# Mixed small edits in a two-branch streaming encoder step: first tiles, weight copies in DRAM, closing norm

## The chip, the cores and the metric

The kernel runs on one core of a Trainium2 chip. The metric is the time of one execution on the device in microseconds (us), lower being better. Engine names are those of the profile: PE is TensorE, DVE is VectorE, ACT is ScalarE, POOL is GpSimd, SP is SyncE, which here only issues transfers. A line such as L1037 is a line of the kernel before.

## The reference

One layer is applied to two independent groups of frames: 512 frames of a new stream (the prompt) and 32 frames of a running one (the sample). Both go through the same weights, so the kernel joins them into 544 columns. Cut to what matters:

```
xn   = rmsnorm(x, norm_g)
proj = xn @ w_in            # u, v, z, gates, q, f, i, g, ga, gb
c    = silu(causal_conv(u));  q, k = c @ w_qm, c @ w_km   (4 heads of 512)
hm   = mLSTM(q, k, v, gates; C, n, m)  -> new C, n, m
oh   = HGRN2(q_h, f_h, i_h; S)         -> new S
y    = sigmoid(ga) * (hm' @ w_brm) + sigmoid(gb) * (oh' @ w_brh)
h    = x + y @ w_out
h    = h + sigmoid(h @ w_pg) * (p @ w_ple)
out  = rmsnorm(h, final_g)
```

All of it is float32. Outputs are out and the new states of both groups.

## The kernel before, in words

Activations lie with features on the 128 partitions and the 544 frames along the free axis, so x is eight tiles of 128 x 544 (KD = 8). To keep float32 precision in matmuls on rounded operands, every operand is split into a high part (a cast) and a low part (a subtraction), and three products are summed: high x high, high x low, low x high. ACT makes most of the high parts, DVE the low parts (split_piece, L127 to L135). Large weight matrices are paired and multiplied with seven in place of eight products (class Two).

The order of the work is set in two ways. In the first stage (L1397 to L1609) the orders of ACT, DVE and PE are those of the code. Behind it only PE's order is that of the code; the builder orders ACT, DVE, POOL and SP itself by its own estimate, within the data dependences. `tc.issue_after(x)` adds one rule: what is issued inside, on x's engine, comes behind x in its queue.

The first stage loops over the eight x tiles (L1413 to L1436). Each tile is scaled by norm_g and split (L1417, L1418), the first three columns of weights are split (wf), the tile is squared into sq for the sum of squares (L1426 or L1428), and products() issues PE's matmuls for the tile two before. ACT squares all tiles but 0 and 2, which POOL squares; POOL also adds the squares of tiles 0 and 1 and of 2 and 3 (L1431), and DVE adds the rest. `summed` is POOL's last of these adds. Behind it in POOL's queue stand the eight scalings of the sample's columns, xg (L1441), and further small copies that name `summed`: the edges of the convolution tiles (conv_edges, L257) and the ones behind the values (L1499, L1608).

The matrices w_out and w_pg are needed late, in sums and differences of their blocks. late_steps() makes these in DRAM: sixteen groups of four transfers of 256 KB each, all issued from POOL's queue, as plain copies or as accumulating ones. make_late(n, after) issues the next n groups, behind an instruction on POOL. Its places are stage_k (L985, behind the ksm copies of the sample's keys), stage_scores (L1024, for heads 0 and 1, behind the scaled queries qw) and the value part of heads 1 to 3. For head 0 that is one group in stage_k and one in stage_scores.

stage_decay reads a tile bc, a row of DRAM broadcast to 128 partitions by SP (decay_rows, L929 to L933). DVE adds the mask to it (dm, L943), POOL copies a piece of it to wi (L953), and qw is the queries times wi. The first score product, sc (L1037), takes a PSUM buffer that vq, the sample's values, had before; DVE's three vsum sums (L1616) read it out.

The last stage runs the w_pg product, adds the gated embeddings to h and squares it into total, in two halves of 272 columns. Then rms_cols takes the sum of squares of a half by six small matmuls (r10 for the first half, r11 for the second) and computes 1/sqrt by a short chain on DVE; norm_bcast spreads the result over the partitions with six matmuls (r1pb); norm_out scales the eight h tiles of that half, five on DVE (L2166) and three, the tiles 4, 5 and 6 called `aside`, on POOL (L2164), and sends each as one y transfer (L2167). Between these, PE makes the last head's new memory C (memories()): three blocks of four steps of six matmuls, then one block in two halves. C leaves through ACT's queue. TAIL says how many steps stand where:

```
next(rest)                        # one step
r = rms_cols(... one ...)         # r10
for _ in range(TAIL[0]): next(rest)
r1 = rms_cols(... other ...)      # r11
norm_out(0, norm_bcast(0, r))
for _ in range(TAIL[1]): next(rest)
norm_out(1, norm_bcast(1, r1))
```

Of the kernel before, what the change touches and what calls it, by code (L numbers as in the profile page):

```python
# [14 lines left out]
ALU = mybir.AluOpType  # L15
# [41 lines left out]
LASTBR = 2  # L57
WSPLIT = 256
U5, U7, U4, U6 = range(4)
TAIL = (4, 4)  # L60
FIRST = 1 << 24

V_FG, V_CW, V_CB, V_MG, V_SK, V_LB, V_HG, V_CS, V_GV = 0, 8, 72, 88, 104, 120, 136, 144, 192
# [4 lines left out]
def hybrid_step(ctx: ExitStack, tc: tile.TileContext, a, o):  # L68
# [29 lines left out]
    def half(b):  # L98
        return slice(b * TH, (b + 1) * TH)
# [126 lines left out]
    def rms_cols(acc, blocks, name, pc=None):  # L226

        pc = pc or paux(name + "pc")
        n = len(blocks)
        st = small("rms_s", [P, 8])  # L230
        V.memset(st[:, :n], 1.0)
        for i, (t0, m) in enumerate(blocks):
            PE.matmul(pc[:m, 0, 2 * i : 2 * i + 2], acc[:, t0 : t0 + m], ones, start=True, stop=True)
        i = 0
        while i < n:
            j = i
            while j < n and blocks[j][1] == blocks[i][1]:
                j += 1
            m = blocks[i][1]
            V.tensor_scalar(st[:m, i:j], pc[:m, 0, 2 * i : 2 * j : 2], 1.0 / D, EPS, ALU.mult, ALU.add)  # L240
            i = j
        r = small("rms_r", [P, 8])
        rsqrt(r[:, :n], st[:, :n], P, n)
        return r
# [169 lines left out]
    def make_late(n, after):  # L414

        with tc.issue_after(after.ins):
            for _ in range(n):
                next(late_sums)
# [545 lines left out]
    def stage_k(h):  # L964

        cs = st8[h]["cs"]
        kf, ks = [], []
        for u in range(2):
            w = st8[h].pop(f"wk{u}", None) or weight(a["w_km"][h, u], f"wk{h}{u}", eng=V if h else G)
            for f in range(2):  # L970
                acc = dense(w, f * P, 256, P, cs, f"k{h}{u}{f}")
                t = eslot(f"kf{h}{u}{f}")
                for b in range(2):
                    with tc.high_priority() if h else nullcontext():
                        read = S.mul(t[:, half(b)], acc[b], HD**-0.5)  # L975
                if u == 0:
                    first = read
                kf.append(t)
                kh, kl = slot(f"kh{h}{u}{f}", F32R), slot(f"kl{h}{u}{f}", F32R)
                n = NP - P if h else NP  # L980
                S.copy(kh[:, :n], t[:, NS : NS + n])
                V.tensor_tensor(kl[:, :n], t[:, NS : NS + n], kh[:, :n].bitcast(F32), ALU.subtract)
                ks.append((kh, kl))
        ksm, copied = triple(kf, "ksm")
        make_late(2 if h > 1 else 1, copied)  # L985
        st8[h].update(kf=kf, ks=ks, ksm=ksm, copied=copied)
        return first

# [28 lines left out]
    def stage_scores(h):  # L1017

        dj, ds, wi, ks, ksm, qs, qf, qw = (st8[h][k] for k in ("dj", "ds", "wi", "ks", "ksm", "qs", "qf", "qw"))
        kf, qx = st8[h]["kf"], st8[h].get("qx")  # L1020
        for i in range(KH):
            scaled = G.tensor_tensor(qw[:, i], qf[:, i * NS : (i + 1) * NS], wi, ALU.mult)
        if h < 2:
            make_late(1, scaled)  # L1024
        sh2, sl2 = slot(f"sh2{h}", F32R), slot(f"sl2{h}", F32R)
        st = []
        for j in range(NB):
            pn = paux(f"sc{h}{j}")
            n = NP - j * P
            for f in range(KH):  # L1030
                if h and j == NB - 1:
                    PE.matmul(
                        pn[:, 0, :n], kf[f][:, T - P : T], qx[:, f], start=(f == 0), stop=(f == KH - 1)
                    )
                    continue
                for i, (x, y) in enumerate(((0, 0), (0, 1), (1, 0))):
                    PE.matmul(  # L1037
                        pn[:, 0, :n],
                        ks[f][x][:, j * P : (j + 1) * P],
                        qs[f][y][:, NS + j * P : T],  # L1040
                        start=(f == 0 and i == 0),
                        stop=(f == KH - 1 and i == 2),
                    )
            with tc.high_priority():
                V.tensor_tensor(dj[j], pn[:, 0, :n], dj[j], ALU.mult)
            if j < 2:
                sh, sl = slot(f"sh{h}{j}", F32R)[:, :n], slot(f"sl{h}{j}", F32R)[:, :n]
            else:
                sh, sl = (x[:, (j - 2) * 256 : (j - 2) * 256 + n] for x in (sh2, sl2))
            with tc.high_priority():  # L1050
                S.copy(sh, dj[j])
                low = V.tensor_tensor(sl, dj[j], sh.bitcast(F32), ALU.subtract)
            st.append((sh, sl))
        pn = paux(f"scs{h}")
        for f in range(KH):
            PE.matmul(
                pn[: 3 * NS, 0, :NS],
                ksm[:, f],
                qf[:, f * NS : (f + 1) * NS],
                start=(f == 0),  # L1060
                stop=(f == KH - 1),
            )
        dss = small("dss", [3 * NS, NS], F32R)
        V.tensor_tensor(ds, pn[: 3 * NS, 0, :NS], ds, ALU.mult)
        V.tensor_copy(dss, ds)
        V.tensor_tensor(dss[2 * NS :], ds[2 * NS :], dss[2 * NS :].bitcast(F32), ALU.subtract)
        st8[h].update(st=st, dss=dss)
        return low
# [328 lines left out]
    with tc.manual_schedule(engines={mybir.EngineType.Activation, mybir.EngineType.DVE, mybir.EngineType.PE}):  # L1397
# [15 lines left out]
        for k in range(KD):  # L1413
            t = xt[k]
            hi, lo = pair_tile(f"x0{k}", k // (KD // 2))
            g = t[:, T : T + 1]
            S.mul(hi, t[:, :T], g)  # L1417
            V.scalar_tensor_tensor(lo, t[:, :T], g, hi.bitcast(F32), ALU.mult, ALU.subtract)  # L1418
            x0.append((hi, lo))
            wf[k].append(split_piece(wf[k][0], f"wf{k}", NF * P))  # L1420
            if k == 1:
                load(KD - 2)
                load(KD - 1)
            sqk = slot(f"r0q{k}")[:, :T]
            if k not in (0, 2):
                S.activation(sqk, t[:, :T], AF.Square)  # L1426
            else:
                G.tensor_tensor(sqk, t[:, :T], t[:, :T], ALU.mult)  # L1428
            sq.append(sqk)
            if k in (1, 3):  # L1430
                summed = G.tensor_tensor(sq[k - 1], sq[k - 1], sqk, ALU.add)  # L1431
            if k in (5, 6):
                i, j = ((0, 2), (4, 5))[k - 5]
                V.tensor_tensor(sq[i], sq[i], sq[j], ALU.add)
            if k > 1:
                products(k - 2)  # L1436
        for i, j in ((0, 4), (6, 7), (0, 6)):
            V.tensor_tensor(sq[i], sq[i], sq[j], ALU.add)
        with tc.issue_after(summed.ins):
            for k in range(KD):  # L1440
                G.tensor_scalar(xg[:, k], xt[k][:, :NS], xt[k][:, T : T + 1], None, ALU.mult)  # L1441
        raws = [raw_piece(a["w_in"][3][:, c : c + WP], f"wu3r{c}") for c in (0, WP)]
        w3 = [split_piece(raws[0], "wu30", WP, WSPLIT)]
        products(KD - 2)
# [701 lines left out]
    def norm_bcast(b, r):  # L2146
        pb = paux(f"r1pb{b}")
        for i, (t0, m) in enumerate(blocks):
            bcast(pb[:, 0, t0 : t0 + m], r, i, m)
        return pb  # L2150
# [7 lines left out]
    def norm_out(b, pb):  # L2158
        rows = slot(f"rows{b}")
        S.copy(rows[:, :TH], pb[:, 0, :TH])  # L2160
        for f in (0, 4, 1, 2, 5, 3, 7, 6):
            t = h1[f][:, half(b)]
            if f in aside:
                G.tensor_tensor(t, t, rows[:, :TH], ALU.mult)  # L2164
            else:
                V.scalar_tensor_tensor(t, t, vcol(V_FG + f), pb[:, 0, :TH], ALU.mult, ALU.mult)  # L2166
            nc.sync.dma_start(o["y"][f, :, half(b)], t)  # L2167

    def memories():
        for f in range(KH - 1):  # L2170
# [4 lines left out]
    with tc.manual_schedule(engines={mybir.EngineType.PE}):  # L2175
        pump = Pump(gates_)
        pump.prepare(2)
        h_sums(HK - 1)
        pump.to(2)
        for f in range(NB):  # L2180
            for i in range(2):
                nc.sync.dma_start(kw[f][i][:, :HD].bitcast(F32), kv_d[f, i, :, :HD])
                nc.sync.dma_start(vv[f][i][:, :VW].bitcast(F32), kv_d[NB + f, i, :, :VW])
        pump.end()
        rest = memories()
        next(rest)
        r = rms_cols(total[0][:, one], blocks, "r10")
        norm_scale()
        for _ in range(TAIL[0]):
            next(rest)  # L2190
        r1 = rms_cols(total[0][:, other], blocks, "r11")
        norm_out(0, norm_bcast(0, r))
        for _ in range(TAIL[1]):
            next(rest)
        norm_out(1, norm_bcast(1, r1))
        for _ in rest:
            pass
# [98 lines left out]
```

## Time and profile before

| | us |
|---|---|
| timed runs | 1104.68, 1108.60, 1108.76 |
| their median | 1108.6 |
| the profiled execution | 1106.54 |
| its span, first to last instruction | 1104.8 |
| PE busy in it | 1093.3 |
| DVE busy | 925.5 |
| ACT busy | 692.7 |
| POOL busy | 210.6 |

The profile is of one execution, whose own time stands in the table beside its span; durations and starts below are from it, counted from the span's start. The granted PE clock is 0.999 of full speed over the span. Rows of the timeline give start, duration, engine, line, operation, output and inputs, shapes and a count; idle time before a row stands in brackets, with what ended it by the profile's guess. Matmuls overlap each other, so a row of one can be longer than the distance to the next.

### The profile page before, as it was taken

The numbers are of one execution on the slowest core, as the hardware profiler recorded it, in microseconds if no ns is written. First come the engines' busy times: TensorE is split into PE (matmuls) and PEld (weight loads), VectorE is DVE, ScalarE is ACT, GpSimd is POOL, SyncE is SP. The second block draws the span as 40 slices with busy tenths as digits, with TensorE's granted clock in tenths as the row PEclk, the third lists the DMA queues.
The fourth block names the chain that finished last, engine by engine and source line by source line (L and its number), as shares of the span: only waits on it lengthen the run. The fifth ranks groups of instructions, "written<-read, shape, count | busy, mean of one in ns | idle before, by whom it ended". The sixth has DMA issues, their size and how long they took to land.

```text
span 1104.8 us, 23775 instructions
## 1 busy us (share of the span) xinstructions
PE 1093.3 (99%) x8625; PEld 1070.3 (97%) x8625; DVE 925.5 (84%) x2101; ACT 692.7 (63%) x1577; POOL 210.6 (19%) x376
## 2 busy tenths in 40 slices
PE   9999999999999999999999999999999999999997
PEld 8899999999999999999999999999999999999997
DVE  7889988676896795986888799999999977778885
ACT  6767557754666554765656477776776666446683
POOL 7204010303021031202220122322232210000001
PEclk9999999999999999999999999999999999999999
DMA  7135325549355377544698666666756683327753
GB/s 231 58 115 181 122 76 166 156 134 207 131 170 172 107 178 176 162 166 155 201 259 253 176 145 142 136 146 150 161 138 153 153 228 102 106 88 243 246 182 121
DMA packets 97550, 176.58 MB, mean 160 GB/s; under 512 B 11284, under 2 KB 18964, under 8 KB 97176
## 3 DMA queue, kind: packets, MB, share of 16 engines
q1 hardware_dynamic: 81504, 141.43, 39.8%
q0 software_dynamic: 15040, 32.51, 16.2%
q8 instruction: 68, 1.11, 0.4%
q10 hardware_dynamic: 888, 1.12, 0.3%
q14 instruction: 50, 0.41, 0.1%
HBM read 150.10 MB, written 41.69 MB: 174 GB/s over the span
## 4 chain that ended last, share of the span: by engine, by line
PE 90%; DVE 5%; DMA 3%; issue 1%; ACT 1%; SPq 0%; POOL 0%; ACTq 0%; DVEq 0%
PE d L608 43%; PE ya L167 9%; PE yb L167 4%; PE k L167 4%; PE q L167 4%; PE C L1077 3%; PE nm L1257 3%; PE pl L1836 2%; PE vp L1580 2%; PE u L291 2%; PE d L460 2%; PE sc L1037 2%; DMA ws<-in_w_in 1%; PE ple L167 1%; PE kt L1122 1%
## 5 line engine op out<-in xcount | busy, mean ns | idle before, releaser
L495 POOL DMA_DIRECT2D ws<-in_w_in x46 | 39.7, 865 | 212.2 <-DVE hkq L1854 47.9
L622 ACT COPY t<-d 128x272 f32<-128x272 f32 x153 | 58.2, 380 | 14.2 <-PE d L608 14.2
L1854 DVE TENSOR_TENSOR hkq<-hkq,q 128x288 f32<-128x288 f32 (+1 forms) x96 | 40.6, 430 | 2.8 <-PE pl L1838 1.0
L785 DVE SCALAR_TENSOR_TENSOR cv<-ub,vec,cv 128x547 f32<-128x547 f32 x48 | 37.6, 782 | 1.6 <-ACT cv L780 1.2
L1836 PE MATMUL pl<-hkq,km 128*128 128x128 f32 x224 | 36.0, 282 | 0.7 <-ACT km L1822 0.7
L1822 ACT COPY km<-hkq 128x256 f32<-128x256 f32 x56 | 24.0, 428 | 14.1 <-DVE hkq L1854 5.4
L1836 PEld LDWEIGHTS pl<-hkq,km 128*128 128x128 f32 x224 | 30.4, 189 | 2.0 <-ACT km L1822 1.6
L1191 DVE SCALAR_TENSOR_TENSOR c<-c,wi,Cs 128x258 f32<-128x258 f32 x32 | 15.3, 479 | 18.7 <-PE Cs L1189 18.4
L1354 DVE TENSOR_TENSOR y<-ya,y 128x272 f32<-128x272 f32 x48 | 18.8, 434 | 12.1 <-PE ya L167 10.2
L1089 ACT COPY Co<-C 128x258 f32<-128x258 f32 x30 | 9.8, 378 | 29.3 <-PE C L1077 27.0
L777 POOL COPY uo<-ub 128x3 f32<-128x3 f32 x16 | 18.7, 1168 | 34.5 <-DVE ub L631 26.6
L1861 DVE COPY_PREDICATED at<-lmask,pl 128x256 f32<-128x256 uint8 (+1 forms) x56 | 25.2, 450 | 0.1
L961 POOL COPY ksm<-kf 128x96 f32<-128x96 f32 x16 | 7.7, 484 | 85.2 <-ACT kf L975 85.0
L1268 ACT COPY y<-nm 128x516 f32<-128x516 f32 x16 | 9.4, 591 | 22.9 <-PE nm L1257 19.8
L133 POOL TENSOR_TENSOR wple50l<-wple5r,wple50h 128x256 fp32r<-128x256 f32 x1 | 0.7, 737 | 120.0 <-ACT wple50h L132 120.0
L961 POOL COPY vsm<-vt 128x96 f32<-128x96 f32 x12 | 5.6, 471 | 86.7 <-ACT vt L633 44.4
L1801 POOL TENSOR_SCALAR_AFFINE_SELECT aa<-at 128x128 f32<-128x128 f32 x32 | 19.6, 645 | 8.1 <-DVE at L1861 8.0
L1245 DVE BATCH_NORM_STATS2 bs<-y 128x6 f32<-128x512 f32 (+1 forms) x20 | 13.8, 691 | 8.2 <-ACT y L1268 8.0
L581 POOL DMA_DIRECT2D ws<-in_w_in x14 | 14.1, 1010 | 32.1 <-DVE ws272l L133 27.6
L1257 PE MATMUL nm<-vhl,sh 128*128 128x258 f32 x112 | 18.4, 286 | 0.0
L376 POOL DMA_DIRECT2D w_pg_d<-in_w_pg x16 | 13.1, 817 | 24.4 <-issue 23.5
L1960 ACT ACTIVATE osq<-kq 128x128 f32<-128x128 f32 x32 | 9.8, 305 | 12.4 <-DVE kq L1955 12.1
(4735 smaller groups left out, 5088.0 us busy)
## 6 DMA issues: line engine op xcount, KB each, us to landing
ws<-in_w_in POOLq DMA_DIRECT2D x60, 256.0 KB, 4.9
ws<-in_w_in SPq DMA_DIRECT2D x46, 256.0 KB, 3.7
ya_d<-y SPq DMA_DIRECT2D x32, 272.0 KB, 2.3
y<-ya_d SPq DMA_DIRECT2D x24, 272.0 KB, 3.3
w_out_d<-in_w_out POOLq DMA_DIRECT2D x24, 256.0 KB, 6.4
w_pg_d<-in_w_pg POOLq DMA_DIRECT2D x24, 256.0 KB, 6.7
c<-in_C SPq DMA_DIRECT2D x16, 258.0 KB, 3.7
out_Cs<-c SPq DMA_DIRECT2D x16, 258.0 KB, 3.4
```

The lines of the kernel that those rows point to most:

```text
L167: PE.matmul(both[b][:m, :TH], part(w, off + k * step, m, x), xx[:, half(b)], start=(k == 0 and j == 0), stop=(k == n - 1 and j == 2),)
L291: PE.matmul(both[b][:m, :TH], part(w, off + k * step, m, x), xx[:, half(b)], start=(k == 0 and j == 0), stop=(k == KD - 1 and j == 2),)
L495: G.dma_start(t, piece(u, i), accum_op=ALU.add)
L608: PE.matmul(ps, ww[:, c], xx, start=(start and k == 0 and j == 0), stop=end, skip_group_check=not start,)
L622: self.kept = S.copy(t, ps)
L785: V.scalar_tensor_tensor(cv[:, :547], ub[:, j : j + 547], vcol(V_CW + 4 * ft + j), cv[:, :547], ALU.mult, ALU.add)
L1077: PE.matmul(pn[g][:, :VH], kw[b][x][:, f * P : (f + 1) * P], vv[b][y][:, g * VH : (g + 1) * VH], start=(b == 0 and j == 0), stop=(b == NB ...
L1257: PE.matmul(pn[:, g, :VH], st[j][x][:, (i - j) * P : (i - j + 1) * P], vv[j][y][:, g * VH : (g + 1) * VH], start=(j == 0 and q == 0), stop ...
L1822: low = S.copy(km.rearrange("p (n j c) -> p n j c", j=2, c=c), view(kk, HB, ((2 * c, NA // (2 * c)), (c - HB, 2), (1, c))),)
L1836: PE.matmul(out, km[:, b * P : (b + 1) * P], view(qq, b * P, dims), start=True, stop=True)
L1854: V.tensor_tensor(x, x, d, ALU.mult)
L1861: V.copy_predicated(at[:, :n], lmask[:, li, :n], pn[:, 0, :n])
```

## The change

It has four edits. In the first stage ACT squares all eight tiles and DVE makes the two sums that POOL made; the xg scalings are no longer placed behind POOL's sum, and `summed` is now the last xg scaling, behind which the small POOL copies stand. In head 0 the first group of DRAM copies moves from behind ksm to behind qw, where two groups now follow each other; heads 1 to 3 keep theirs. In the last stage the steps of C are dealt out anew. And the second half's y tiles 4, 5 and 6 are sent from POOL's queue; all other y stay on SP's.

```diff
-TAIL = (4, 4)
+TAIL = (2, 3, 2, 2)
...
-        make_late(2 if h > 1 else 1, copied)
+        make_late((0, 1, 2, 2)[h], copied)
...
         if h < 2:
-            make_late(1, scaled)
+            make_late(2 - h, scaled)
...
-            if k not in (0, 2):
-                S.activation(sqk, t[:, :T], AF.Square)
-            else:
-                G.tensor_tensor(sqk, t[:, :T], t[:, :T], ALU.mult)
+            S.activation(sqk, t[:, :T], AF.Square)
             sq.append(sqk)
             if k in (1, 3):
-                summed = G.tensor_tensor(sq[k - 1], sq[k - 1], sqk, ALU.add)
+                V.tensor_tensor(sq[k - 1], sq[k - 1], sqk, ALU.add)
...
-        with tc.issue_after(summed.ins):
-            for k in range(KD):
-                G.tensor_scalar(xg[:, k], xt[k][:, :NS], xt[k][:, T : T + 1], None, ALU.mult)
+        for k in range(KD):
+            summed = G.tensor_scalar(xg[:, k], xt[k][:, :NS], xt[k][:, T : T + 1], None, ALU.mult)
...
-            nc.sync.dma_start(o["y"][f, :, half(b)], t)
+            (nc.gpsimd if b and f in aside else nc.sync).dma_start(o["y"][f, :, half(b)], t)
...
-        next(rest)
+        for _ in range(TAIL[0]):
+            next(rest)
         r = rms_cols(total[0][:, one], blocks, "r10")
         norm_scale()
-        for _ in range(TAIL[0]):
+        for _ in range(TAIL[1]):
             next(rest)
         r1 = rms_cols(total[0][:, other], blocks, "r11")
+        for _ in range(TAIL[2]):
+            next(rest)
         norm_out(0, norm_bcast(0, r))
-        for _ in range(TAIL[1]):
+        for _ in range(TAIL[3]):
             next(rest)
         norm_out(1, norm_bcast(1, r1))
```

## The prediction

> **What bounds the kernel now.** I read the page first, then the list of waits for TensorE alone, then the timeline at the places that list names, and last the transfers and time windows there.
>
> ```profile
> span 1104.8 us, 23775 instructions
> PE 1093.3 (99%) x8625; PEld 1070.3 (97%) x8625; DVE 925.5 (84%) x2101; ACT 692.7 (63%) x1577; POOL 210.6 (19%) x376
> ```
>
> TensorE (PE) is busy for 1093.3 of 1104.8 us, and no edit takes a matmul away. Only the missing 11.5 us can be won: the lead-in, the stretch after the last matmul, and PE's waits. Of these there are few; the columns are total, times, longest:
>
> ```profile
> PE u L291 <- DVE wf1l L133: 0.8, 1, 0.8
> PE r1pb L248 <- DVE rms_r L181: 0.8, 1, 0.8
> PE sc L1037 <- DVE vsum L1616: 0.7, 1, 0.7
> PE r10pc L233 <- DVE pg L2130: 0.6, 1, 0.6
> PE kt L1122 <- DVE kwl L1127: 0.3, 1, 0.3
> ```
>
> The first belongs to the first tiles, the third and fifth to head 0's scores and values, the second and fourth to the closing norm. The change's three parts stand beside exactly these places, so each part is priced by the waits it can reach.
>
> **Part 1, the first tiles.** POOL loses two squares and two sums; ScalarE (ACT) gains the squares, VectorE (DVE) the sums. A timeline row is start, duration, engine, line, operation, and in brackets the idle time before it:
>
> ```profile
> 7.77 1.15 POOL L1428 TENSOR_TENSOR r0q<-x 128x544 f32<-128x544 f32 x1 [2.19 <-DMA x<-in_xT]
> 7.88 1.45 DVE L133 TENSOR_TENSOR wf1l<-wf1r,wf1h 128x384 fp32r<-128x384 f32 x1
> 8.88 1.66 POOL L1431 TENSOR_TENSOR r0q<-r0q,r0q 128x544 f32<-128x544 f32 x1
> 9.26 1.87 DVE L1418 SCALAR_TENSOR_TENSOR x<-x,x 128x544 fp32r<-128x544 f32 x1
> 9.39 0.39 PE L291 MATMUL u<-x,wf1l 128*128 128x272 f32 x1 [0.82 <-DVE wf1l L133]
> 10.11 0.65 ACT L1426 ACTIVATE r0q<-x 128x544 f32<-128x544 f32 x1
> 11.05 0.55 DVE L133 TENSOR_TENSOR wf2l<-wf2r,wf2h 128x384 fp32r<-128x384 f32 x1
> 12.93 6.20 POOL L1441 TENSOR_SCALAR xg<-x 128x32 f32<-128x32 f32 x6
> 13.96 0.80 DVE L1418 SCALAR_TENSOR_TENSOR x<-x,x 128x544 fp32r<-128x544 f32 x1
> 16.32 0.73 DVE L1434 TENSOR_TENSOR r0q<-r0q,r0q 128x544 f32<-128x544 f32 x1
> 10.00:20.00 10.00, 10.00 (x81) 9.86 (x80) 10.00 (x14) 8.49 (x18) 10.00 (x14) 1.00 0.93 310
> ```
>
> The same DVE subtraction takes 1.45 us beside POOL's square and 0.55 without; the same scaling 1.87 beside POOL's sum and 0.80 without. At 0.55, wf1l ends 0.90 sooner, at 8.43. PE's 0.82 at 9.39 waited for just that, so all of it can go. Afterwards PE is busy for all of the window from 10 to 20 us (the second number of the last row; DVE and ACT are the fourth and fifth), so what it wins it keeps if DVE and ACT keep pace. DVE's ledger: 2 x 0.73 = 1.46 more, against 0.90 at wf1l and 1.07 at the next scaling, 1.97 less. ACT's: 2 x 0.65 more. The first square falls where ACT waits for the second tile's load; the second pushes the rest back by 0.65, and ACT is idle for 1.51 of that window.
>
> The eight xg scalings on POOL no longer queue behind POOL's sum, and the edge copies queue behind the last xg instead. Six xg take 6.20 us, 1.03 each, and the DVE scaling among them still takes 0.80: they get out of DVE's way. If one caught wf1l and held it for its whole 1.03, nothing would be won. I take 0.8, by the row at 13.96, with ends of 0 and 0.9.
>
> The Trainium skill has a rule for such a pair, SBUF — State Buffer, section "SBUF: two separate sides": a DVE instruction with two SBUF inputs and a GpSimd instruction that reads SBUF exclude each other, and whoever starts first holds the ports throughout. The 1.45 beside 0.55 agrees. By it an early xg may win the ports too, and then this term would be nearer to 0.
>
> **Part 2, the DRAM copies.** Head 0's first group of four w_out copies leaves its place behind the ksm copies and goes with the second group behind qw. The groups stay sixteen; no DMA is added.
>
> ```profile
> 90.67 2.38 POOL L372 DMA_DIRECT2D w_out_d<-in_w_out  x4
> 91.24 0.84 SPq L932 DMA_DIRECT2D bc<-nm_d  x2
> 98.05 0.21 POOL L953 COPY wi<-bc 128x32 f32<-128x32 f32 x1 [4.77 <-ACT q L1005]
> 98.12 0.29 DVE L943 TENSOR_TENSOR dm<-bc,cmask 128x128 f32<-128x128 f32 x1 [2.21 <-PE q L167]
> 101.38 2.10 POOL L372 DMA_DIRECT2D w_out_d<-in_w_out  x4
> 102.51 0.73 PE L1037 MATMUL sc<-q,kh 128*128 128x512 f32 x2 [0.69 <-DVE vsum L1616]
> 106.64 0.38 SPq L932 DMA_DIRECT2D bc<-nm_d  x1
> 111.39 0.28 POOL L953 COPY wi<-bc 128x32 f32<-128x32 f32 x1 [7.91 <-DMA bc<-nm_d]
> ```
>
> The row broadcast bc leaves SP at 91.24, right beside the four copies, and its first readers on POOL and on DVE start at 98.05 and 98.12, 6.8 us after. The profile blames ACT and PE, but two engines that begin within 0.07 us on the same tile point to the tile. The third broadcast took 111.39 - 106.64 = 4.75. DVE is idle for 2.21 ahead of dm; the vsum sums stand behind dm in its queue, and the last one releases PE at 102.51. Without the copies I put bc at 91.24 + 4.75 = 96.0, 2.1 earlier, and PE's 0.69 has nothing left to wait for. The kt wait of 0.3 hangs on the same queue. I take 0.7, by the row of the third broadcast, with ends of 0 (the blame was right) and 1.0.
>
> What is pushed back: at 101.38 eight copies go out in place of four, the last four 2.4 us later than now, and POOL's next work is the wi copy at 111.39. The copy of r that stands behind the four now comes 2.4 earlier; the list shows no wait of PE for it. What the burst does to other loads is rival B.
>
> **Part 3, the closing norm.** PE's new order is two steps of C, r10, three steps, r11, two, first broadcast, two, second broadcast; it was one, r10, four, r11, first broadcast, four, second. A step is six matmuls.
>
> ```profile
> 1084.98 3.08 PE C L1077 x24
> 1087.90 0.64 PE L233 MATMUL r11pc<-ones,pg 128*128 128x2 f32 x6
> 1089.34 1.00 PE L248 MATMUL r1pb<-ident,rms_r 128*128 128x128 f32 x6 [0.80 <-DVE rms_r L181]
> ```
>
> Four steps take 3.08, a step 0.75. The extra step covers the 0.6 in front of r10, whose input is ready when it was. r11 then comes at 1084.98 + 3 x 0.75 = 1087.2, 0.7 earlier, and the first broadcast after 0.64 and two more steps, at 1089.3. It waited for r, and r's last steps stood on DVE behind r11's first, which waited for PE; that is 0.7 sooner, so r is due near 1088.6 and the 0.80 goes. The second broadcast is due two steps after the first, not four. PE ends 0.6 + 0.8 = 1.4 earlier, but the first y leaves when it did, because the first broadcast does. So the outputs decide:
>
> ```profile
> 1091.64 9.47 SPq L2167 DMA_DIRECT2D out_y<-h  x16
> 1095.60 1.92 SPq L2167 DMA_DIRECT2D out_y<-h  x1
> 1094.75 2.24 POOL L2164 TENSOR_TENSOR h<-h,rows 128x272 f32<-128x272 f32 x3 [1.67 <-ACT rows L2160]
> 1096.66:1098.00 1.34, 1.34 (x14) 1.34 (x12) 0.17 (x1) 0.52 (x2) 0.33 (x1) 1.00 0.05 11
> 1098.00:1102.66 4.66, 1.48 (x13) 1.27 (x11) 0.00 (x0) 0.75 (x2) 0.00 (x0) 1.00 1.03 352
> out_y<-h SPq DMA_DIRECT2D x16, 136.0 KB, 3.0
> ws<-in_w_in POOLq DMA_DIRECT2D x60, 256.0 KB, 4.9
> L495 POOL DMA_DIRECT2D ws<-in_w_in x46 | 39.7, 865 | 212.2 <-DVE hkq L1854 47.9
> ```
>
> The window rows end in DMA share and GB/s: while SP's ninth issue takes 1.92, the transfer engines stand nearly empty for 1.34 us, then run full until 1102.66. Three paths lead to the end:
> - SP issues 13 y, not 16. Without the long one an issue takes (9.47 - 1.92) / 15 = 0.50, so it is done 1.5 earlier, also if the 1.92 stays; nothing shows that it goes.
> - POOL alternates three products of 0.75 with three issues. The nearest row is the ws load, 0.87 to issue and 4.9 to land. From 1094.75 - 1.4 that gives 1093.35 + 3 x 1.62 + 4.9 = 1103.1. SP's last y lands now at 1101.1 + 3.0 = 1104.1, so this path ends 1.0 earlier, and 2.9 earlier if it lands in y's own 3.0.
> - Transfers: POOL's y can fill the 1.34 hole, which brings the last byte 1.3 forward; C's outputs, from an earlier PE, help at the start.
>
> I take 1.4, between the three, with ends of 0.1 (hole and slow landing both stay) and 2.5.
>
> **The sum.** 0.8 + 0.7 + 1.4 = 2.9 us. The profiled execution took 1106.5 us, 1.7 around its span, and would take 1103.6. The timed runs are 1104.68, 1108.6 and 1108.76, median 1108.6; that is 2.1 above the profiled one, and the mean of the four is 1107.1. I take the mean as the level and forecast 1107.1 - 2.9 = 1104.2 us. A difference below 0.5%, 5.5 us, is about what a measurement of this kernel cannot tell from none.
>
> **The rivals.**
> A, the tail stays as long as its transfers: the bytes are the same, the hole returns with SP's ninth issue and POOL's y land late. For it: a share of 1.03 after the hole. Against it: 11 GB/s in the hole, which a second queue can use. The tail gives 0.3, the sum is 1.8, the time 1105.3. The Trainium skill speaks for A in DMA: Bandwidth & Descriptors, section "Issuing engines are not separate DMA queues": all issuers share the 16 engines, and a second one only saves issue time. Here the issue time is part of what ends last, so the row of the hole speaks the other way.
>
> B, slower: the eight copies in a row collide with head 0's state loads, and the sample product waits.
>
> ```profile
> 116.71 0.90 SPq L1145 DMA_DIRECT2D c<-in_C  x2
> c<-in_C SPq DMA_DIRECT2D x4, 258.0 KB, 3.1
> 120.87 1.00 PE L1203 MATMUL nm<-c,qw 128*32 128x258 f32 x8
> ```
>
> The last c goes out by 117.2 and lands 3.1 later, at 120.3, 0.6 before PE needs it. If it landed only after 7.6 us, bc's 6.8 stretched by the larger burst, PE would stand for 7.6 - 3.1 - 0.6 = 3.9, and the time is 1107.1 - 2.9 + 3.9 = 1108.1, slower than before. It decides when the burst still runs at 117. Against it: the four copies at 90.67 and the two broadcasts, together some 7 us of transfers up to bc's 98.05, are as much as the burst holds beyond what runs there now; eight copies from 101.38 should be through by about 113.
>
> C, the first tiles win nothing, because an xg takes the POOL square's place beside wf1l. The sum is 2.1, the time 1105.0. Against it is the 0.80 at 13.96; for it, the rule on the ports in part 1.
>
> D, all upper ends: 0.9 + 1.0 + 2.5 = 4.4, the time 1102.7. It needs PE's end to be what ends last, and the long SP issue to go.
>
> That the change does not do what it says can be left out: fixed engine orders and named queues are what it edits, apart from the order of DVE, ACT and POOL behind the first stage, which the builder picks anew and which may move either way.
>
> **How the numbers follow.** Forecast 0.45, A 0.2, B 0.08, C 0.12, D 0.1, and 0.05 for another order that costs more than it brings. The range goes from 1100.2, D's 4.4 from the fastest run shown, to 1108.1, B. Faster by over 0.5% means under 1103.1 against the median of 1108.6; the forecast misses that by 1.1, about half of how far the runs shown lie from their mean, so I give it 0.28: D, a third of the forecast's share, and a little of the rest. Slower by over 0.5% is reached by no case that is named: 0.05. That leaves 0.67.
>
> **What would show it.** In the new profile: wf1l near 0.55 and no wait of PE at 9 us; dm on DVE near 96 and no wait at sc; no wait at r10pc and r1pb, the second broadcast 2.5 after the first; transfers without a hole, the last byte 2.9 earlier. I am wrong if a new wait over 1 us stands anywhere in the list, if bc still takes over 6 us, or if a y from POOL lands last.

## The result, and the profile after

| | kernel before | changed kernel |
|---|---|---|
| median of 22 runs each, us | 1105.87 | 1104.02 |
| lowest and highest | 1104.34 to 1108.76 | 1102.57 to 1105.67 |
| ratio, 95% interval | | 0.9981 [0.9974, 0.9987] |
| span of the profiled execution | 1104.8 | 1101.5 |

By the ratio the change wins 0.19%, 2.1 us (1.4 to 2.9); the two medians differ by 1.85. That is no difference at the 0.5% of the prediction, and one that the interval of many runs tells from zero. The forecast of 1104.2 is within 0.2 us, but its level was 1.2 too high (1107.1 for the kernel before, against 1105.87) and its gain 0.8 too large (2.9), or 1.0 by the medians. The two errors nearly cancel: that the time came out so near is luck. The two profiled spans differ by 3.3, more than the runs do: a single pair of executions overstates this change.

TensorE's whole list of waits in the changed kernel (total, times, longest) is three rows:

```profile
PE warm L1403 <- DVE emc L1239: 1.1, 1, 1.1
PE pl L1832 <- ACT km L1818: 0.5, 1, 0.5
PE yt L1307 <- DVE y L1296: 0.2, 1, 0.2
```

All five waits at which the prediction aimed are gone, and no new one over 1 us has come: the 1.1 stands in every profile of this study, that of the kernel before too.

The first tiles, from the timeline:

```profile
7.05 0.93 POOL L1437 TENSOR_SCALAR xg<-x 128x32 f32<-128x32 f32 x1 [0.82 <-DMA x<-in_xT]
7.28 0.56 DVE L133 TENSOR_TENSOR wf1l<-wf1r,wf1h 128x384 fp32r<-128x384 f32 x1
7.74 0.74 DVE L1428 TENSOR_TENSOR r0q<-r0q,r0q 128x544 f32<-128x544 f32 x1
8.40 0.78 DVE L1418 SCALAR_TENSOR_TENSOR x<-x,x 128x544 fp32r<-128x544 f32 x1
8.49 1.30 POOL L1437 TENSOR_SCALAR xg<-x 128x32 f32<-128x32 f32 x1 [0.51 <-DMA x<-in_xT]
```

wf1l takes 0.56 where it took 1.45, and a scaling 0.78 where one took 1.87, although an xg runs on POOL beside each. An xg started 0.23 before wf1l and did not hold it; the ones paying are the xg themselves (0.93 and 1.30, where the one before them, with no DVE work beside it, took 0.37).

The copies and head 0's broadcast:

```profile
89.26 0.85 SPq L932 DMA_DIRECT2D bc<-nm_d  x2
93.80 0.57 POOL L953 COPY wi<-bc 128x32 f32<-128x32 f32 x1 [4.63 <-DMA bc<-nm_d]
94.22 0.30 DVE L943 TENSOR_TENSOR dm<-bc,cmask 128x128 f32<-128x128 f32 x1
99.78 4.47 POOL L372 DMA_DIRECT2D w_out_d<-in_w_out  x8
103.64 0.77 SPq L932 DMA_DIRECT2D bc<-nm_d  x1
105.70 8.91 SPq L1145 DMA_DIRECT2D c<-in_C  x4
112.79 0.21 POOL L953 COPY wi<-bc 128x32 f32<-128x32 f32 x1 [8.55 <-DMA bc<-nm_d]
117.90 0.98 PE L1203 MATMUL nm<-c,qw 128*32 128x258 f32 x8
```

The broadcast's first reader starts 4.54 after its issue (6.81 before), and dm on DVE no longer stands idle ahead of it. The third broadcast now sits in the burst of eight copies and takes 9.15 (4.75 before); nothing of PE waits for that. The sample product nm starts at 117.90, 3.0 earlier than before, without a wait.

The closing norm:

```profile
1079.54 0.29 PE L608 MATMUL d<-h,ws4107l 128*128 128x272 f32 x1
1081.19 0.71 PE L233 MATMUL r10pc<-ones,pg 128*128 128x2 f32 x6
1084.10 0.64 PE L233 MATMUL r11pc<-ones,pg 128*128 128x2 f32 x6
1086.32 1.00 PE L248 MATMUL r1pb<-ident,rms_r 128*128 128x128 f32 x6
1088.62 8.02 SPq L2163 DMA_DIRECT2D out_y<-h  x13
1088.80 0.92 PE L248 MATMUL r1pb<-ident,rms_r 128*128 128x128 f32 x6
1094.91 0.34 ACTq L1108 DMA_DIRECT2D out_Cp<-Co  x1
1097.40 0.34 ACTq L1108 DMA_DIRECT2D out_Cp<-Co  x1
```

The second broadcast comes 2.5 after the first, as forecast. The number to read is another one: from the gates' last matmul (first row) to the first y it is 9.08 us; before, 1082.63 to 1091.64, it was 9.01. The first y leaves when it did, and what follows it is a full transfer system. Time windows, ending in DMA share and GB/s:

```profile
1088.60:1090.00 1.40, 1.40 (x12) 1.25 (x12) 1.31 (x4) 0.44 (x2) 1.40 (x2) 1.00 0.39 136
1090.00:1098.00 8.00, 4.95 (x42) 4.74 (x40) 2.13 (x5) 1.55 (x5) 4.07 (x7) 1.00 0.98 334
1098.00:1100.00 2.00, 0.00 (x0) 0.00 (x0) 0.00 (x0) 0.00 (x0) 0.00 (x0) 0.50 0.28 91
```

The hole of 1.34 us is filled. Yet the span ends 12.88 after the first y (13.16 before), and 6.83 after the start of PE's last matmul (5.61 before): PE ends 1.43 sooner against the gates, and 1.2 of that is given back. The issues with their median time to landing:

```profile
out_y<-h SPq DMA_DIRECT2D x13, 136.0 KB, 4.2
out_Cp<-Co ACTq DMA_DIRECT2D x3, 258.0 KB, 2.7
out_y<-h POOLq DMA_DIRECT2D x3, 136.0 KB, 4.1
out_Cp<-Co ACTq DMA_DIRECT2D x2, 129.0 KB, 4.3
```

A y took 3.0 to land before and 4.2 now, on either queue: with the transfer engines at a share of 0.98 they queue behind each other. POOL's last y was issued at 1094.02, and SP's later ones landed after it.

### The profile page after: what moved, and what is told of

It is laid out like the page before. It is cut to its first block, busy times and chain, and to the rows that moved or that the text cites. A ratio compares the mean times of both kernels' runs of the same rounds, so it can differ in the third digit from the quotient of the medians.

```text
span 1101.5 us, 23773 instructions
## 1 busy us (share of the span) xinstructions
PE 1092.4 (99%) x8625; PEld 1070.9 (97%) x8625; DVE 922.8 (84%) x2103; ACT 693.1 (63%) x1579; POOL 209.5 (19%) x375
## 4 chain that ended last, share of the span: by engine, by line
PE 93%; DMA 3%; DVE 2%; issue 1%; SPq 0%; ACT 0%; POOL 0%; ACTq 0%; POOLq 0%
PE d L608 44%; PE ya L167 9%; PE yb L167 4%; PE q L167 4%; PE k L167 4%; PE C L1077 4%; PE nm L1257 3%; PE sc L1037 2%; PE pl L1832 2%; PE u L291 2%; PE d L460 2%; PE vp L1576 2%; DMA ws<-in_w_in 1%; PE ple L167 1%; PE kt L1122 1%; PE ht L1902 1%
```

## The experiments

Twelve kernels ran. Each ratio is against the kernel before on the same chip, with its 95% interval. First each edit alone, from the kernel before.

**Part 1 alone.** ACT makes all squares, DVE the two sums, xg is free.

```diff
-            if k not in (0, 2):
-                S.activation(sqk, t[:, :T], AF.Square)
-            else:
-                G.tensor_tensor(sqk, t[:, :T], t[:, :T], ALU.mult)
+            S.activation(sqk, t[:, :T], AF.Square)
...
```

> Only the first tiles' edit. The profile after shows PE 1.6 us earlier at the sum of squares (21.27 against 22.89), where 0.8 was forecast. Theory: POOL's two-input instructions slowed DVE, and PE waited for DVE; the time falls by 1.0 to 1.6 us. Rival: half of the 1.6 is an earlier load of the second tile in that one execution, and the time falls by about 0.8 us. Second rival: the win is lost again before 100 us, and the time stays.

Measured 1106.39, ratio 1.0001 [0.9991, 1.0012]: the second rival's outcome. PE starts its 600th matmul 1.05 earlier and has lost 0.66 of that by the 900th:

```profile
97.62 0.21 POOL L953 COPY wi<-bc 128x32 f32<-128x32 f32 x1 [5.57 <-DMA bc<-nm_d]
102.13 0.73 PE L1037 MATMUL sc<-q,kh 128*128 128x512 f32 x2 [0.92 <-DVE vsum L1612]
```

The broadcast left at 89.76 and reached its reader 7.86 later; the score product waits 0.92, more than the 0.69 before. The broadcast took 1.05 longer than before in this execution, which used up most of the earlier start.

**Part 2 alone.** The first group of copies moves behind qw.

```diff
-        make_late(2 if h > 1 else 1, copied)
+        make_late((0, 1, 2, 2)[h], copied)
...
-            make_late(1, scaled)
+            make_late(2 - h, scaled)
```

> Only the moved group of DRAM copies. The profile after shows another 1.4 us between 92 and 120 us, where 0.7 was forecast. Theory: the copies delayed the broadcast bc, and DVE with it; bc's readers start under 5 us after its issue, PE's wait at the scores goes, and the time falls by 0.7 to 1.4 us. Rival: DVE and POOL waited for PE and ACT, as the profile names them; then dm starts no earlier against PE's q, and the time stays. Second rival: the burst of eight copies delays head 0's states, and PE waits at the sample product.

Measured 1104.53, ratio 0.9987 [0.9979, 0.9996], 1.4 us faster, as the theory said. The first reader starts 4.43 after the broadcast's issue, and from the 600th to the 900th matmul PE needs 1.40 less.

**The closing order alone.** All y stay on SP.

```diff
-TAIL = (4, 4)
+TAIL = (2, 3, 2, 2)
...
-        next(rest)
+        for _ in range(TAIL[0]):
+            next(rest)
         r = rms_cols(total[0][:, one], blocks, "r10")
...
```

> Only the new order of PE's closing matmuls, all y on SP. Theory: PE ends 1.4 us earlier, but SP still issues sixteen y and the end moves by at most 0.5 us. Rival: the end follows PE, and the time falls by 1.4 us.

Measured 1105.31, ratio 0.9996 [0.9987, 1.0004]: the theory. The rival's 1.4 us lies at the edge of the interval, and the profile speaks against it: PE's last matmul follows the gates 1.43 sooner than before, the span's end 0.29 sooner.

**The queue alone.** Three y of the second half go from POOL.

```diff
-            nc.sync.dma_start(o["y"][f, :, half(b)], t)
+            (nc.gpsimd if b and f in aside else nc.sync).dma_start(o["y"][f, :, half(b)], t)
```

> Only the three y from POOL's queue, PE's closing order as before. Theory: SP's queue was what ended last, and the time falls by 1.0 to 1.6 us also without the new order. Rival: the last C output, which waits on ACT's queue for a y to land, ends last, and the time falls by under 0.5 us.

Measured 1105.9, ratio 1.0005 [0.9997, 1.0014]: nothing, so the theory's 1.0 to 1.6 us are out.

Then pairs and what is left when one piece is taken out.

**Parts 1 and 2.** The first two diffs of this section together.

> Parts 1 and 2 of the change (first tiles' squares, and the DRAM copies behind the scaled queries), the closing norm as before. Alone, part 1 gave a ratio of 1.0001 and part 2 of 0.9987. Theory: part 1 starts the work 0.8 to 1.0 us earlier, and this is lost at the scores as long as the bc broadcast (7.8 us after its issue) lands behind the copies; with the copies moved it is kept. Then the two together give 2.2 to 2.5 us, a ratio of 0.9978 to 0.9981, and the matmul that starts at 129.9 us before starts 2.5 to 3.0 us earlier. Rival: the earlier start is absorbed by a later weight load anyway; then the ratio is that of part 2, 0.9987.

Measured 1104.47, ratio 0.9987 [0.9979, 0.9996]: the ratio of part 2 alone, so the rival's number, though the interval also holds the theory's 0.9979 to 0.9981. Its profile also shows something else, told at the end.

**Part 3 whole.** The third and the fourth diff together.

> Part 3 whole (closing norm's order and three y from GpSimd's queue), the first tiles and copies as before. Alone, the order gave 0.9996 and the queue 1.0005. Theory: each needs the other: with the order alone SyncE's sixteen y are last, with the queue alone TensorE is; together they give 0.3 to 0.8 us, a ratio of 0.9993 to 0.9997, less than the 1.45 us by which TensorE ends earlier, because the last C output, on ScalarE's queue, is issued only when one of SyncE's y has landed. Rival: the two effects only add: 1.0001.

Measured 1105.99, ratio 0.9999 [0.9990, 1.0007]: neither theory can be told from the other at this size, and both are small.

**The change without POOL's y.**

```diff
-            (nc.gpsimd if b and f in aside else nc.sync).dma_start(o["y"][f, :, half(b)], t)
+            nc.sync.dma_start(o["y"][f, :, half(b)], t)
```

> The changed kernel with all sixteen y on SyncE's queue again. Theory: SyncE's issue of sixteen y, with its one long issue, ends the kernel then, as with the order alone: 0.3 to 0.8 us slower than the changed kernel, 0.9985 to 0.9989 against the kernel before. Rival: the transfers themselves bound the end (about 350 GB/s from the first y on); then the queue that issues doesn't matter and the ratio is that of the changed kernel, 0.9981.

Measured 1103.74, ratio 0.9978 [0.9970, 0.9987]. Sixteen y on one queue are no slower than thirteen and three: the rival. The theory's 0.9985 to 0.9989 begins inside the interval, but three pairs of kernels differ by the queue alone (1.0005 against 1, 0.9999 against 0.9996, 0.9981 against 0.9978), and in none does POOL's queue win anything.

**The change with the last C from POOL's queue.**

```diff
-            nc.scalar.dma_start(o["Cp"][h, f][:, c], co[:, c])
+            nc.gpsimd.dma_start(o["Cp"][h, f][:, c], co[:, c])
```

> The changed kernel with the two halves of the last C output sent from GpSimd's queue, not from ScalarE's. Theory: in the changed kernel the last half was ready at 1095.7 us and issued at 1097.40, when a y with which it shared a semaphore had landed; from the other queue it isn't held, and pays 0.6 us for its issue and 4.1 for the landing: last byte 0.5 to 1.0 us earlier, a ratio of 0.9972 to 0.9977 against the kernel before. Rival 1: the transfers bound the end: no change, 0.9981. Rival 2: GpSimd's slower issue and landing cost more than the hold: 0.9984 or more.

Measured 1103.89, ratio 0.9980 [0.9970, 0.9990]: no change. The last C is not held any more, and the end does not move for it; in the profile SP's last y goes out later instead, 17.4 after the gates and not 16.3, and the span ends 13.32 after the first y. My theory, that one held transfer made the end, finds no support, though its 0.9972 to 0.9977 are inside the interval.

**The change with half of each y.** It sends 136 of the 272 columns of each piece and leaves the other half of y out.

```diff
-            (nc.gpsimd if b and f in aside else nc.sync).dma_start(o["y"][f, :, half(b)], t)
+            (nc.gpsimd if b and f in aside else nc.sync).dma_start(o["y"][f, :, slice(b * TH, b * TH + TH // 2)], t[:, : TH // 2])
```

> The changed kernel, but each of the sixteen y transfers sends only the first half of its 272 columns (this leaves half of y out), so that the number of issues and the order stay and 1.1 MB of 3.0 MB after the first y are gone. Three kernels with the new order end 6.7 to 7.3 us after TensorE's last matmul, whichever queue sends (6.7 with sixteen y on SyncE, 6.8 with three on GpSimd, 7.3 with the last C there too), the kernel before 5.6. Theory: the transfers, at some 350 GB/s from the first y on, bound the end, and the waits for a semaphore are only how that shows: with half the bytes the last C is issued when it is ready and the end comes 1.2 to 2.5 us earlier, a ratio against the kernel before of 0.9957 to 0.9970. Rival: the number of issues at 0.5 us each and the long ninth one bound it, whatever the bytes: 0.9976 to 0.9981, as the changed kernel.

Measured 1102.06, ratio 0.9959 [0.9946, 0.9973]. Same issues, same order, 1.1 MB less: 11.47 from the first y to the end, not 12.88, and a y lands in 3.0 again.

```profile
out_y<-h SPq DMA_DIRECT2D x13, 68.0 KB, 3.0
out_Cp<-Co ACTq DMA_DIRECT2D x2, 129.0 KB, 3.0
```

The bytes bound the tail of the changed kernel, which rules the rival out. By an estimate, 1.1 MB at the 334 GB/s of the window above are 3.3 us, and 1.41 of them went: with half the bytes something else ends last, which was not followed.

**The second half's norm moved behind the first half's broadcast.** If the end follows the first y, bring that forward.

```diff
-        for _ in range(TAIL[1]):
+        for _ in range(4):
             next(rest)
-        r1 = rms_cols(total[0][:, other], blocks, "r11")
-        for _ in range(TAIL[2]):
-            next(rest)
         norm_out(0, norm_bcast(0, r))
-        for _ in range(TAIL[3]):
+        r1 = rms_cols(total[0][:, other], blocks, "r11")
+        for _ in range(3):
             next(rest)
```

> The changed kernel with the second half's norm moved behind the first half's broadcast: two C blocks, the first half's sums, four blocks, its broadcast and y, then the second half's sums, three blocks, its broadcast. In the changed kernel VectorE interleaves the two halves' inverse roots: between two steps of the first half's it waited 0.9 us for the second half's sums, and the first y was issued at 1088.6. Theory (the transfers bound the end from the first y on): the first half's root is done some 1.0 us earlier, the first y goes out 0.8 to 1.3 us earlier and the kernel ends 0.5 to 1.0 us earlier than the changed one, 0.9969 to 0.9976 against the kernel before, unless the second half's y, 1.5 to 2 us later then, leave the transfers a hole. Rival: that hole, or a later last C, takes it all back: 0.9979 to 0.9985.

Measured 1104.85, ratio 0.9983 [0.9975, 0.9992]: the rival. The first y came 8.14 after the gates, 0.94 sooner, but PE then stood for 2.27 in front of the second broadcast, and after that ran at half its clock (the clock is the third number from the end of the window):

```profile
1092.00 1.00 PE L248 MATMUL r1pb<-ident,rms_r 128*128 128x128 f32 x6 [2.27 <-DVE rms_r L185]
```

```profile
1090.00:1092.00 2.00, 0.00 (x0) 0.03 (x1) 1.54 (x11) 0.00 (x0) 0.00 (x0) 1.00 1.00 354
1094.00:1096.00 2.00, 2.00 (x11) 2.00 (x11) 1.59 (x4) 0.00 (x0) 2.00 (x4) 0.50 0.29 102
```

**The change without part 1.** The first diff is undone, the rest of the change stays.

> The changed kernel without part 1: the first tiles' squares and sums as before; copies, closing order and queue as changed. In the profiled executions the kernels with part 1 started their 150th matmul 1.30 us (mean of five, 1.05 to 1.61) before the kernel before's, those without it 0.31 (mean of five, -0.13 to 0.70). Theory: that 1.0 us is kept to the end once the copies are moved: this kernel is 0.7 to 1.0 us slower than the changed one, 0.9987 to 0.9990 against the kernel before. Rival: part 1 is worth nothing at the end, as alone (1.0001): 0.9978 to 0.9983.

Measured 1104.25, ratio 0.9980 [0.9972, 0.9989]: the rival. Its profile starts the 600th matmul 1.4 later than the changed kernel's, and yet its ratio is not above that kernel's 0.9981. The interval still reaches into the theory's 0.9987 to 0.9990.

**The two inverse roots one after the other.** In the changed kernel DVE's order holds the first half's root up for a step of the second half's, which waits for PE:

```profile
1083.71 0.16 DVE L184 SCALAR_TENSOR_TENSOR rsq_u<-rsq_u,rms_s 128x3 f32<-128x3 f32 x1
1084.77 0.16 DVE L240 TENSOR_SCALAR rms_s<-r11pc 128x2 f32<-128x2 f32 x1 [0.90 <-PE r11pc L233]
1084.85 0.15 DVE L185 SCALAR_TENSOR_TENSOR rms_r<-rsq_u,rms_r 128x3 f32<-128x3 f32 x1
```

```diff
-TAIL = (2, 3, 2, 2)
+TAIL = (2, 3, 1, 4)
...
-            V.tensor_scalar(st[:m, i:j], pc[:m, 0, 2 * i : 2 * j : 2], 1.0 / D, EPS, ALU.mult, ALU.add)
+            with tc.issue_after(after.ins) if after is not None else nullcontext():
+                V.tensor_scalar(st[:m, i:j], pc[:m, 0, 2 * i : 2 * j : 2], 1.0 / D, EPS, ALU.mult, ALU.add)
...
-        r1 = rms_cols(total[0][:, other], blocks, "r11")
+        r1 = rms_cols(total[0][:, other], blocks, "r11", after=rooted[0])
```

Here `rooted[0]` is the last instruction of the first root.

> The changed kernel with the closing norm's two inverse roots one after the other on VectorE (the first step for the second half's sums waits for the first half's root), the first broadcast one C block earlier and the second two blocks after where it stood relative to it. In the kernels before and after the change alike, the first y goes out 9.0 us after the gates' last matmul, and everything has landed 11.9 to 12.4 us after that first y, whichever queues send and wherever TensorE ends. Theory (the end follows the first y, behind which 3.0 MB go out at some 350 GB/s): VectorE no longer stands still for 0.9 us inside the first root, the first y goes out 0.7 to 1.1 us earlier, 7.9 to 8.3 us behind the gates, and the kernel ends as much earlier than the changed one: 0.9970 to 0.9976 against the kernel before, still 11.9 to 12.1 us after its first y. Rival: the end follows TensorE's last matmul by 6.0 us, which stays where it was: 0.9978 to 0.9983, and first y to the end grows to 12.8 us or more.

Measured 1103.13, ratio 0.9967 [0.9954, 0.9980], the fastest kernel of the study that does all of the work, some 3 us faster than before (3.0 by the medians, 3.6 by the ratio of six runs); its interval overlaps that of the changed kernel. The first y leaves 8.17 after the gates, as the theory said, and the end comes 21.37 after them, 0.59 sooner than in the changed kernel, though PE now waits again and ends 1.0 later. Two rows of it, the second broadcast and a window behind it:

```profile
1090.95 1.00 PE L251 MATMUL r1pb<-ident,rms_r 128*128 128x128 f32 x6 [0.97 <-DVE rms_r L187]
```

```profile
1092.00:1096.00 4.00, 4.00 (x34) 4.00 (x35) 2.13 (x5) 1.40 (x4) 3.45 (x5) 1.00 0.70 240
```

The expected constant held: counted to the last landing, as the expectation counts, it is 12.04 after the first y. In the changed kernel the same count gives 11.71, and to the span's end it is 13.20 here against 12.88. So about 0.3 of the 0.91 won at the first y is given back: the second half's y come later, and the transfers run at 240 GB/s for 4 us. The rival is out, since PE ends later and the kernel sooner. The end follows the first y only while the queue behind it stays full; in the kernel with the late second norm, where it did not, the span ends 15.21 after the first y.

All profiles side by side, in us. Columns: the start of PE's 600th matmul against the kernel before; the stretch from there to the 900th, likewise; from there to the gates' last matmul, likewise; from the gates to the span's end, in full.

```
kernel                     600th   to 900th   to gates   gates to end
before                      0        0          0          22.17
1 alone                    -1.05    +0.66      +0.28       22.18
2 alone                    -0.70    -1.40      +0.33       21.94
order alone                -0.36    +0.06      +0.29       21.88
queue alone                +0.13    -1.34      +0.48       22.10
1 and 2                    -1.24    -1.18      +2.04       22.85
3 whole                    -0.65    -1.33      +0.85       22.00
1, 2 and order             -1.06    -1.44      +0.99       21.78
2 and 3                    -0.19    -1.18      -0.30       21.94
changed kernel             -1.61    -1.39      -0.09       21.96
last C from POOL           -1.54    -1.44      +1.64       22.41
half of y                  -1.25    -1.45      -0.19       20.56
late second norm           -1.47    -1.44      +0.12       23.36
roots in turn              -1.13    -1.43      -0.04       21.37
```

## Why the prediction was right, and where its terms were not

**Part 1, 0.8 forecast: right at its place, not shown at the end.** The mechanism stands in the rows: wf1l at 0.56, no wait at 9 us. The 0.8, though, was that of one execution. In the six kernels without part 1 PE waited for wf1l 0.8, 0.8, 0.5 and 0.5, and twice not at all: once POOL's square began only after wf1l (part 2 alone), once PE got there later (part 3 whole). That is 0.4 on average. Over the eight kernels that have it the 600th matmul starts 1.29 earlier on average, over the six without it 0.30: 1.0 us, above the forecast; what the rest of it comes from was not followed.

But the medians do not show it. Three pairs differ by part 1 alone, and their ratios by +0.0001, 0.0000 and +0.0001 (part 1 against the kernel before; 1 and 2 against 2; the changed kernel against 2 and 3); 0.8 us would be -0.0007 in each. One pair could miss that, three leave it little room. The step that failed is "what it wins it keeps if DVE and ACT keep pace". Between the 900th matmul and the gates, where no edit lies, the executions differ by 2.3 us. Part of that stands at late weight loads. In the window from 690 to 716 us the split of one, ws451h on ACT, waits for its load. The first row is of the changed kernel, the second of the one without POOL's y, which loses 0.7 there:

```profile
ACT ws451h L132 <- DMA ws<-in_w_in: 0.9, 1, 0.9
```

```profile
ACT ws451h L132 <- DMA ws<-in_w_in: 2.3, 1, 2.3
```

Three kernels wait 2.3 or 2.4 there, and PE loses 0.7 to 0.8 in each; in the other eleven ACT waits 1.6 at most, and PE loses no more than 0.1. That the early start of part 1 is lost at such loads is argued, not shown.

Rival C is refuted in its mechanism, no xg held wf1l, though its price, nothing for part 1, is what the medians give. The Trainium skill's rule on the shared ports, in SBUF — State Buffer, section "SBUF: two separate sides", agreed with wf1l's 1.45 beside POOL's square; here the xg that had started first did not block wf1l (0.56 beside 0.55 without POOL), and the measurement decides. Five POOL squares that began 0.11 to 0.22 before wf1l each stretched it to 1.45; four xg that began 0.10 to 0.23 before it left it at 0.55 or 0.56.

**Part 2, 0.7 forecast: mechanism right, its size too small.** The blame was wrong as the prediction read it, and bc was late. The nine kernels with the copies moved start the first reader 3.9 to 5.2 after the issue, the five without 5.1 to 7.9. PE waited at sc, for 0.7 to 0.9, in the three kernels whose reader started 6.8 to 7.9 after the issue, and in none of those at 5.4 or less. The stretch from the 600th to the 900th matmul is 1.18 to 1.45 shorter in all nine. Without the move it was as short in two of five executions (queue alone, part 3 whole). In those two the broadcast left 0.13 and 0.16 after the first of the four copies, in the other three 0.24 to 0.57 after it; that this distance decides was not tried. So the edit makes sure of a case that otherwise comes and goes: 1.37 against 0.39 on average, 1.0 us. By medians it is worth 0.0013 alone, 0.0014 with part 1 and 0.0019 with part 3, 1.4 to 2.1 us. Two waits, 0.7 and 0.3, were the whole list the term was built on, and its upper end of 1.0 held too little, as the three medians have it; the interval of part 2 alone, 0.4 to 2.3 us, holds the 0.7 as well. Rival B did not come: the burst stretched the third broadcast to 9.15 and PE waited for none of it.

**Part 3, 1.4 forecast: the step on the outputs failed.** PE's part is exact: its end comes 1.40 to 1.44 sooner behind the gates in all seven kernels with just the new order. The prediction also had the first y leave when it did. What failed is "I take 1.4, between the three": the third path, the transfers, set the end. In the five kernels with the new order and their full outputs, the last C on ACT's queue, the end follows the gates by 21.78 to 22.00, in the four with the old order and a full clock by 21.94 to 22.18: 0.2 us, whichever queue sends. That is rival A's tail (0.3), for a reason that it named: the bytes are the same. Its other reason, the hole, was wrong: the hole went, and each y took 1.2 longer to land instead. It went for the most part with the order alone: there, with all y on SP, it lasted 0.6 and not 1.34 us, and a y took 3.3. The rule that the prediction set aside is the one that held: the Trainium skill, DMA: Bandwidth & Descriptors, section "Issuing engines are not separate DMA queues". With 16 engines at a share of 0.98 for 8 us, three issues on another queue are worth nothing (0.9978 without them, 0.9981 with), and half the bytes are worth 1.4 us by the profiles' tails and 2.4 by the medians (0.9959 against 0.9981). Two of the prediction's landing times were also added to an issue's end, where the page counts from its start: SP's last y landed at 1103.66 before, not at 1104.1, and POOL's path was put 0.9 too long. The step does not hang on that.

**The sum.** Forecast 0.8 + 0.7 + 1.4 = 2.9. By the stretches of the profiles 1.0 + 1.0 + 0.2 = 2.2, by medians about 0 + 1.7 + 0.5 (part 3 as the mean of 0.0001, 0.0006 and 0.0007). Measured 2.1. The total was near because a term too small stood beside one too large (two, by the medians), and the time nearer still because the level of four runs was 1.2 off: that is luck, not the working. The range's lower end is 1104.68 - 4.4 = 1100.3, not 1100.2. How the 1.7 to 2.0 of the first two divides between them stays open.

## What to carry to other kernels

When the last stage is mostly output, measure from the first output transfer to the end: if that is bytes over the transfer rate, shorten the way to the first output and leave the compute engine's end alone, but keep the queue behind it full. A transfer that is on the critical path should have no bulk copy issued beside it; such a clash can hide in a profile, because it comes in some executions and not in others. The same goes for a wait: here PE's for wf1l stood in four of six. Price a gain by the stretch in which it lies over several kernels' profiles, since single spans here differed by more than the gain.

## What was not expected of the hardware

**The clock fell after short gaps, once.** In the kernel with parts 1 and 2 PE waited 0.6 and 0.8 us in the closing norm, as in the kernel before, and then ran at half its clock for about 3 us:

```profile
1088.00:1089.00 1.00, 0.20 (x4) 0.13 (x3) 0.77 (x8) 0.00 (x0) 0.00 (x0) 1.00 0.56 219
1091.00:1092.00 1.00, 1.00 (x6) 1.00 (x6) 1.00 (x4) 0.00 (x0) 1.00 (x3) 0.50 0.00 0
```

It cost 1.46: PE's last matmul comes 18.02 after the gates, not 16.56. All five profiles with the old order have these two waits, and one of them shows it; of the seven in which the new order left no wait there, none. The kernel with the roots in turn waited 0.97 and kept its full clock. So what made it fall is open. Whether the order edit earns something by that was not tried. The Trainium skill, TensorE: Matmul & The Clock Gate, section "HAM oscillation — how this bites in real kernels", warns of idle gaps of more than about 3.4 us; here gaps of 0.6 and 0.8 were followed by it once, and one of 2.27 in the kernel with the late second norm.

**A queue can stand still for another queue's transfer.** SP's and ACT's transfers share eight semaphores in turn, and one waits until the earlier one on its semaphore has landed. In the changed kernel the last half of C was ready at 1095.7 and went out at 1097.40, when the y issued at 1092.02 on the same semaphore had landed. Where the transfers are the bound, as here, this only shows the bound.
